# Three turns of normalised rows held back by order edges on TensorE, and the final norm's weights multiplied in together with its scaling on half the columns

## The chip, the cores and the metric

The kernel runs on one core of one Trainium2 chip. The metric is the device time of one execution in microseconds. The engines are TensorE (PE in the profile; PEld is its weight load), VectorE (DVE), ScalarE (ACT), GpSimd (POOL) and SyncE (SP); DMAs are issued from SP, ACT and POOL.

## The reference, cut to what matters

A decoder layer on 256 tokens of 1024 features in float32: an FFN, a token mixer and a second FFN, each behind a norm that is shifted and scaled by a conditioning vector, each added to the residual stream `h` with a gate, and a norm at the end.

```python
def rmsnorm(x, g):
    y = xf * lax.rsqrt(jnp.mean(xf * xf, axis=-1, keepdims=True) + EPS)
    return (y * g.astype(jnp.float32)).astype(x.dtype)

def modulate(n, shift, scale):
    return n * (1 + scale) + shift

def swiglu(n, w_gate, w_up, w_down):
    return (jax.nn.silu(n @ w_gate) * (n @ w_up)) @ w_down

        n = modulate(rmsnorm(h, g_ffn1[l]), sh1, sc1)
        h = h + 0.5 * gt1 * swiglu(n, w1_gate[l], w1_up[l], w1_down[l])
        n = modulate(rmsnorm(h, g_mix[l]), sh2, sc2)
        h = h + gt2 * hybrid_mixer(n, w_in[l], w_pool[l], pool_scale[l], w_out[l])
        n = modulate(rmsnorm(h, g_ffn2[l]), sh3, sc3)
        h = h + 0.5 * gt3 * swiglu(n, w2_gate[l], w2_up[l], w2_down[l])
    return rmsnorm(h, g_final)
```

The mixer projects the normed rows with `w_in`, feeds half the columns to causal pooling and the rest to dilated attention, and projects the result with `w_out`.

## The kernel before, in words

The 256 tokens are two token tiles of 128 rows, t = 0 and 1. `h` lies in SBUF with tokens on the partitions, 1024 columns per tile.

**Products.** A float32 product is made as three products of rounded parts: each weight half of 1024 columns is cast to `hi` on ScalarE (L289) and the remainder to `lo` on VectorE (L290), each activation is split into a high part (`nh`, `hh`, `nhy`) and a low part (`nl`, `hl`, `nly`), and high x hi, low x hi, high x lo are added up in PSUM. Weights come in one stream of 1 MB tiles that SP issues (L273); `want` fetches up to five tiles ahead of the products (`AHEAD`). The conditioning matrix comes in the same stream, and VectorE reduces it (L278).

**The norms in the middle.** When the last product of a tile's accumulator pair has run, `norm_rows` multiplies both accumulators with the gate (L331), adds them to `h` (L333), sums the squares on ScalarE (L336) and VectorE (L339), takes the power -0.5 on GpSimd (L342), and scales the rows into two tiles `xs`, the first on ScalarE (L344), the second on VectorE (L345). Then `norm_mod` turns the rows on TensorE (`turn`, L317: 4 transposes for each half), and ScalarE writes the scaled and shifted columns as `nh` (L363) and `n32` (L364), from which VectorE makes `nl` (L366). This happens four times: for t = 0 and 1 after the first FFN (tags `b0`, `b1`) and after the mixer (tags `c0`, `c1`).

**Where the turns stand.** While tile 0's norm is made, TensorE works on tile 1, and the other way round. The turn of `b0` is recorded among the down products of tile 1 (`ffn_rest`, L509, ahead of the last chunk, `TURN = 3`), that of `c0` among tile 1's products of `w_out` (`wout`, L796), that of `c1` among tile 0's first FFN products (L838), that of `b1` among tile 0's second chunk of the mixer's projection (L775, `AFTER1`). The framework's scheduler then orders each engine's queue by priority and by its own estimate of when things are ready; `norm_mod` runs under a high priority (`urgent`), so it may draw a turn ahead of products recorded before it. An engine works through its queue in the order that the built program gives it. `order_dep(late, early)` adds an edge that only the scheduler sees: `late` gets its place behind `early`, without a semaphore.

**The end.** `finish3(t)` makes the last norm for a tile. `add` multiplies the accumulator with the gate into the scratch `o` (L856) and adds it to `h` (L857). For tile 1 the last 256 columns have a second part, `far` (L444, L869). `square` takes squares and their sum on ScalarE (L861), adds on GpSimd (L862), and multiplies `h` with the final norm's weights `gfb` into `o` (L863). VectorE squares the last 256 columns (L871), GpSimd takes the power (L874), VectorE multiplies the last columns with the weights meanwhile (L875). Then `o` is scaled by the power: columns 0 to 192 and 192 to 640 on VectorE (L877), 640 to 1024 on ScalarE (L879), and three DMAs carry them out (L878 from SP, L880 from ACT). Tile 0's end runs beside tile 1's last products; tile 1's comes after everything.

Of the kernel before, what the change touches and what calls it, by code (L numbers as in the profile page):

```python
# [15 lines left out]
P = 128  # L16
S = 256
NT = S // P
D = 1024
# [26 lines left out]
SPIN = (4, 8, 8, 5)  # L46
SPLIT = (9, 10)
PARTS = 11
PAD = 336
# [122 lines left out]
def block_kernel(ctx, tc, w, vec, x, c, gf, wpool, bandd, biasd, out):  # L172
# [139 lines left out]

    def turn(src, name):

        pt = psp.tile([P, 4, P], F32, name=name, tag="ps")
        for i in range(4):
            nc.tensor.transpose(pt[:, i, :], src[:, ts(i, P)], ident)  # L317
        return pt
# [30 lines left out]

    def norm_mod(xs, which, shm, tag, t=None, xT=None):  # L350

        nh, nl = new_n(tag)
        with urgent(), in_order() as last:
            for b in range(2):
                pt = turn(xs[b], f"xt{tag}{b}")
                if xT is not None and b == 1:
# [69 lines left out]
    def down(f, ci, t, hid, accs, banks=(0, 1)):  # L426
        hi, lo = want("down", (f, ci))
        hh, hl = hid
        for k in range(2):
            first, last = ci == 0 and k == 0, ci == NCH - 1 and k == 1  # L430
            for (a, ww, st, sp) in ((hh, hi, first, False), (hl, hi, False, False), (hh, lo, False, last)):
                for b in banks:
                    mm(accs[b], a[:, k, :], cols(ww, 2 * k + b), start=st, stop=sp)  # L433

# [32 lines left out]
    def lead_step(f, j, n, items, banks, tt=range(NT)):  # L467

        hi, lo = want("lead", (f, j))
        passes = ((0, hi), (1, hi), (0, lo))  # L470
        end = KD - 1 if f == 1 else KD // 2 - 1
        if j % (end + 1) < end:
            steps = [(p, ci, t) for p in range(3) for ci in items for t in tt]
        else:
            steps = [(p, ci, t) for ci in items for t in tt for p in range(3)]
        for p, ci, t in steps:
            a, ww = passes[p]
            last = j == KD - 1 or (ci, j) in ((2, end), (3, end))
            mm(banks[ci][t], n[t][a][:, j, :], cols(ww, lead_set(f, j).index(ci)), start=j == 0 and p == 0,  # L479
               stop=last and p == 2)  # L480

# [5 lines left out]
    def ffn_rest(f, ci0, n, prev, pci, accs, finish, gate):  # L487
# [17 lines left out]
        down(f, NCH - 1, 0, hid[NCH - 1][0], accs[0])  # L505
        after = finish(0)
        for banks in ((0, 1),) if f == 0 else ((0,), (1,)):
            for ci in last:
                if after and ci == last[TURN]:  # L509
                    after()  # L510
                if f == 0 or banks == (0,) or ci < SPLIT[0]:
                    down(f, ci, 1, hid[ci][1], accs[1], banks)
        if f == 1:
# [118 lines left out]
    def finish1(t):  # L632
        with urgent():
            if t == 0:
                scale_cols(1, SC2)
            xs = norm_rows(t, f"b{t}", nm["acc"][t], nm["g"],
                           (place["win", (1, 1)] + 0.5 if t == 0 else place["win", (3, 0)], place["win", (1, 0)] + 1))
        def after():
            nm[t] = norm_mod(xs, 1, SH2, f"b{t}")
            if t == 1:  # L640
# [152 lines left out]

    def wout(t, banks, after=None):
        for n, i in enumerate(WOUT):
            if after and n == TURN1:  # L796
                after()
            hi, lo = want("wout", i)
            yh, yl = y[t]
            for kk in range(2):  # L800
                k = 2 * i + kk
                for (a, ww, st, sp) in ((yh, hi, n + kk == 0, False), (yl, hi, False, False),
                                        (yh, lo, False, n == 3 and kk == 1)):
                    for b in banks:
                        mm(acc2[t][b], a[:, k, :], cols(ww, 2 * kk + b), start=st, stop=sp)  # L805

    n3 = {}

    def finish2(t):
        with urgent():  # L810
            if t == 0:
# [3 lines left out]
                           (place["lead", (1, 4)], place["lead", (1, 2)]))  # L815
        def after():
            n3[t] = norm_mod(xs, 2, SH3, f"c{t}", t, xT3)
            if t == 1:
# [15 lines left out]
    for t in range(NT):  # L834
        for ci in range(LEAD):
            lead[ci][t] = (psp if ci > 1 else accp).tile([P, 512], F32, name=f"le{t}{ci}", tag="ps" if ci > 1 else "acc")
        for j in range(KD // 2):
            if t == 0 and j == TURN2:  # L838
                after()
            lead_step(1, j, n3, range(LEAD), lead, (t,))  # L840
    for j in range(KD // 2, KD):
# [7 lines left out]
    def finish3(t):  # L849
        with urgent():  # L850
# [3 lines left out]

            def add(src, a, b):
                nc.vector.tensor_tensor(o[:, a:b], src, g[:, a:b], ALU.mult)  # L856
                nc.vector.tensor_tensor(ht[:, a:b], ht[:, a:b], o[:, a:b], ALU.add)  # L857

            def square(n, a, b, more):
                sq = work.tile([P, 512], F32, name=f"sqo{t}{a}", tag="t2", bufs=T2)  # L860
                nc.scalar.activation(sq[:, 0:b - a], ht[:, a:b], AF.Square, accum_out=ss[:, n:n + 1])  # L861
                nc.gpsimd.tensor_tensor(ss[:, n:n + 1], ss[:, n:n + 1], more, ALU.add)  # L862
                nc.vector.tensor_tensor(o[:, a:b], ht[:, a:b], gfb[:, a:b], ALU.mult)  # L863
# [10 lines left out]
            nc.gpsimd.tensor_tensor(r, ss[:, 2:3], mhalf, ALU.pow)  # L874
            nc.vector.tensor_tensor(o[:, 768:D], ht[:, 768:D], gfb[:, 768:D], ALU.mult)  # L875
            for a, b in ((0, 192), (192, 640)):
                nc.vector.tensor_scalar(o[:, a:b], o[:, a:b], r, None, ALU.mult)  # L877
                nc.sync.dma_start(out[t * P:(t + 1) * P, a:b], o[:, a:b])  # L878
            nc.scalar.activation(o[:, 640:D], o[:, 640:D], AF.Copy, scale=r)  # L879
            nc.scalar.dma_start(out[t * P:(t + 1) * P, 640:D], o[:, 640:D])  # L880

# [40 lines left out]
```

## Time and profile before

| | |
|---|---|
| median of 3 runs | 486.09 us (485.42 to 486.2) |
| the profiled execution | 485.93 us |
| its span, first to last instruction | 484.1 us |
| mean granted TensorE clock | 0.997 |
| busy: PE, DVE, ACT, POOL | 472.5, 357.8, 261.7, 14.9 us |

In the rows of a timeline the first number is the start in us from the span's start, the second the length, then engine, line, operation, output<-inputs, sizes and count; in brackets stand the idle time of the engine just before it and what ended it. Several like instructions are merged (x8). Matmuls are pipelined, so a row may be longer than the distance to the next one.

### The profile page before, as it was taken

The page shows a single profiled execution, that of the slowest core. Times are in us where ns is not written, and L with a number is a line of the kernel's source. Part 1 is how long each engine was busy: PE and PEld are TensorE (multiplying, and loading weights), DVE is VectorE, ACT ScalarE, POOL GpSimd, SP SyncE. Part 2 cuts the span into 40 slices and gives each one's busy share as a digit, 9 for nine tenths or more (in the row PEclk, how much of TensorE's full clock was granted, in tenths as well). Part 3 has the DMA queues.
Part 4 walks back from the last instruction along what each step waited for, and adds up shares of the span by engine and source line. Part 5 has one row for each costly group of instructions (what it writes and reads, how often), then busy time and mean ns, then how long its engine had stood idle before and what let it go on. Part 6 is the DMA issues. An engine that isn't in the chain of part 4 may idle for free.

```text
span 484.1 us, 6040 instructions
## 1 busy us (share of the span) xinstructions
PE 472.5 (98%) x2188; PEld 382.6 (79%) x2188; DVE 357.8 (74%) x579; ACT 261.7 (54%) x447; POOL 14.9 (3%) x35
## 2 busy tenths in 40 slices
PE   8999999999999999999999999999999999999994
PEld 4778888888888888788778777888878888888883
DVE  4988899996897893699999869866576765655245
ACT  3786595453464451996876388746543643444111
POOL 2000000000000000110001000000000000000010
PEclk9999999999999999999999999999999999999998
DMA  8998895998988791679786963996356757530102
GB/s 303 400 347 348 330 366 191 359 417 330 376 319 328 296 383 79 236 253 383 286 339 238 339 253 104 367 347 227 135 214 260 262 202 319 208 141 0 43 1 87
DMA packets 19215, 126.05 MB, mean 260 GB/s; under 512 B 2329, under 2 KB 3121, under 8 KB 4850
## 3 DMA queue, kind: packets, MB, share of 16 engines
q1 hardware_dynamic: 17568, 121.25, 65.9%
q0 software_dynamic: 1184, 3.98, 2.3%
q10 hardware_dynamic: 434, 0.45, 0.3%
q8 instruction: 17, 0.28, 0.2%
q14 instruction: 12, 0.10, 0.0%
HBM read 124.61 MB, written 1.06 MB: 260 GB/s over the span
## 4 chain that ended last, share of the span: by engine, by line
PE 91%; DVE 3%; ACT 2%; issue 1%; DMA 1%; POOL 1%; POOLq 0%; DVEq 0%; ACTq 0%
PE accf L433 23%; PE gu L394 9%; PE gu L392 9%; PE gu L393 9%; PE le L479 8%; PE ld L479 8%; PE accm L805 4%; PE zp L392 3%; PE zp L394 3%; PE zp L393 3%; PE ht L419 2%; PE yt L731 1%; DMA h<-in_x_dram 1%; PE sh L394 1%; PE ld L394 1%
## 5 line engine op out<-in xcount | busy, mean ns | idle before, releaser
L290 DVE TENSOR_TENSOR lo<-raw,hi 128x1024 fp32r<-128x1024 f32 (+1 forms) x156 | 184.2, 1208 | 43.1 <-ACT hi L289 34.7
L289 ACT CAST hi<-raw 128x1024 fp32r<-128x1024 f32 (+1 forms) x156 | 158.7, 1047 | 70.0 <-DMA raw<-in_w_dram 28.5
L278 DVE CUSTOM_DVE_ANT_0 raw<-raw,cb,vecs 128x1024 f32<-128x1024 f32 x70 | 88.2, 1280 | 1.2 <-DMA raw<-in_w_dram 1.2
L433 PE MATMUL accf<-hi,hh 128*128 128x512 f32 x172 | 54.5, 394 | 0.2
L433 PE MATMUL accf<-hi,hl 128*128 128x512 f32 x172 | 54.4, 391 | 0.0
L433 PE MATMUL accf<-lo,hh 128*128 128x512 f32 x172 | 53.9, 389 | 0.0
L392 PE MATMUL gu<-hi,nhc 128*128 128x512 f32 x112 | 44.4, 396 | 0.0
L410 ACT ACTIVATE sg<-gu 128x256 f32<-128x256 f32 x24 | 9.2, 382 | 64.4 <-PE gu L394 64.4
L394 PE MATMUL gu<-lo,nhc 128*128 128x512 f32 x112 | 43.7, 390 | 0.0
L393 PE MATMUL gu<-hi,nlc 128*128 128x512 f32 x112 | 43.6, 389 | 0.0
L433 PEld LDWEIGHTS accf<-hi,hl 128*128 128x128 f32 x172 | 32.1, 188 | 7.2 <-DVE hl L310 0.7
L433 PEld LDWEIGHTS accf<-lo,hh 128*128 128x128 f32 x172 | 32.3, 188 | 6.8
L433 PEld LDWEIGHTS accf<-hi,hh 128*128 128x128 f32 x172 | 31.7, 188 | 7.2 <-ACT hh L309 1.1
L413 DVE TENSOR_TENSOR pr<-sg,gu 128x256 f32<-128x256 f32 x24 | 10.1, 419 | 33.0 <-ACT sg L410 32.8
L392 PE MATMUL gu<-hi,nha 128*128 128x512 f32 x80 | 31.7, 396 | 0.0
L394 PE MATMUL gu<-lo,nha 128*128 128x512 f32 x80 | 31.2, 390 | 0.0
L393 PE MATMUL gu<-hi,nla 128*128 128x512 f32 x80 | 31.1, 389 | 0.0
L310 DVE TENSOR_TENSOR hl<-ht,hh 128x256 fp32r<-128x256 f32 x44 | 16.4, 418 | 14.4 <-ACT hh L309 14.4
L309 ACT CAST hh<-ht 128x256 fp32r<-128x256 f32 x44 | 14.1, 379 | 23.0 <-PE ht L419 23.0
L392 PE MATMUL zp<-hi,nhb 128*128 128x512 f32 x64 | 26.3, 411 | 0.0
L394 PE MATMUL zp<-lo,nhb 128*128 128x512 f32 x64 | 25.3, 395 | 0.0
L393 PE MATMUL zp<-hi,nlb 128*128 128x512 f32 x64 | 25.1, 392 | 0.0
(194 smaller groups left out, 729.4 us busy)
## 6 DMA issues: line engine op xcount, KB each, us to landing
raw<-in_w_dram SPq DMA_DIRECT2D x112, 1024.0 KB, 5.9
raw<-in_w_dram SPq DMA_DIRECT2D x4, 512.0 KB, 7.8
gt<-gd POOLq DMA_DIRECT2D x3, 512.0 KB, 6.7
h<-in_x_dram SPq DMA_DIRECT2D x2, 512.0 KB, 4.6
bias<-in_bias_dram POOLq DMA_DIRECT2D x2, 512.0 KB, 3.4
band_all<-in_band_dram POOLq DMA_DIRECT2D x1, 544.0 KB, 3.8
gfb<-in_gf_dram POOLq DMA_DIRECT2D x1, 512.0 KB, 12.8
out_dram<-o SPq DMA_DIRECT2D x2, 224.0 KB, 2.4
```

The lines of the kernel that those rows point to most:

```text
L278: note(nc.vector.tensor_tensor_reduce(r, r, cb, 1.0, vecs[:, m:m + 1], ALU.mult, ALU.add, mod[:, m:m + 1]), i, 1)
L289: note(nc.scalar.copy(hi[:, o:o + n], src), i + s / 2, 0)
L290: note(nc.vector.tensor_tensor(lo[:, o:o + n], src, hi[:, o:o + n].bitcast(F32), ALU.subtract), i + s / 2, 0)
L309: nc.scalar.copy(hi_ap, src)
L310: nc.vector.tensor_tensor(lo_ap, src, hi_ap.bitcast(F32), ALU.subtract)
L392: mm(ps, nh[:, k, :], whi, start=first, stop=False)
L393: mm(ps, nl[:, k, :], whi, start=False, stop=False)
L394: mm(ps, nh[:, k, :], wlo, start=False, stop=last)
L413: nc.vector.tensor_tensor(pr, sg, ps[:, 256:512], ALU.mult)
L433: mm(accs[b], a[:, k, :], cols(ww, 2 * k + b), start=st, stop=sp)
L479: mm(banks[ci][t], n[t][a][:, j, :], cols(ww, lead_set(f, j).index(ci)), start=j == 0 and p == 0, stop=last and p == 2)
L805: mm(acc2[t][b], a[:, k, :], cols(ww, 2 * kk + b), start=st, stop=sp)
```

## The change

`turn` takes a list of matmuls and ties each of its transposes behind the 26th of them (`GATE = 25`). `ffn_rest`, `wout` and the first loop of the second FFN collect the products that they issue (`down`, `lead_step` and `wout` now keep them), and hand the list to the turns of `b0`, `c0` and `c1`. `b1`'s turn gets no list (`after(steps=())`). In `finish3` the sum of columns 512 to 1024 is made in two instructions of 256, the products with `gfb` for columns 512 to 1024 are gone, and the last scaling takes them in: VectorE makes `h` x power x `gfb` for columns 512 to 768 and 768 to 1024 in one instruction each, ScalarE scales columns 0 to 512, and the DMAs follow those columns.

```diff
+GATE = 25
...
-    def turn(src, name):
+    def turn(src, name, steps=()):
...
-            nc.tensor.transpose(pt[:, i, :], src[:, ts(i, P)], ident)
+            one = nc.tensor.transpose(pt[:, i, :], src[:, ts(i, P)], ident)
+            if steps:
+                order_dep(one.ins, steps[GATE].ins, "rows are ready later")
...
-                pt = turn(xs[b], f"xt{tag}{b}")
+                pt = turn(xs[b], f"xt{tag}{b}", steps)
...
+        steps = []
         for banks in ((0, 1),) if f == 0 else ((0,), (1,)):
             for ci in last:
                 if after and ci == last[TURN]:
-                    after()
+                    after(steps)
                 if f == 0 or banks == (0,) or ci < SPLIT[0]:
-                    down(f, ci, 1, hid[ci][1], accs[1], banks)
+                    steps += down(f, ci, 1, hid[ci][1], accs[1], banks)
...
-            def add(src, a, b):
+            def add(src, a, b, pieces=1):
                 nc.vector.tensor_tensor(o[:, a:b], src, g[:, a:b], ALU.mult)
-                nc.vector.tensor_tensor(ht[:, a:b], ht[:, a:b], o[:, a:b], ALU.add)
+                for i in range(pieces):
+                    q = slice(a + (b - a) // pieces * i, a + (b - a) // pieces * (i + 1))
+                    nc.vector.tensor_tensor(ht[:, q], ht[:, q], o[:, q], ALU.add)
...
-                nc.vector.tensor_tensor(o[:, a:b], ht[:, a:b], gfb[:, a:b], ALU.mult)
...
-            add(nm["acc"][t][1], 512, D)
+            nc.vector.tensor_tensor(o[:, 0:512], ht[:, 0:512], gfb[:, 0:512], ALU.mult)
+            add(nm["acc"][t][1], 512, D, 2)
...
-            nc.vector.tensor_tensor(o[:, 768:D], ht[:, 768:D], gfb[:, 768:D], ALU.mult)
-            for a, b in ((0, 192), (192, 640)):
-                nc.vector.tensor_scalar(o[:, a:b], o[:, a:b], r, None, ALU.mult)
+            for a, b in ((512, 768), (768, D)):
+                nc.vector.scalar_tensor_tensor(o[:, a:b], ht[:, a:b], r, gfb[:, a:b], ALU.mult, ALU.mult)
                 nc.sync.dma_start(out[t * P:(t + 1) * P, a:b], o[:, a:b])
-            nc.scalar.activation(o[:, 640:D], o[:, 640:D], AF.Copy, scale=r)
-            nc.scalar.dma_start(out[t * P:(t + 1) * P, 640:D], o[:, 640:D])
+            nc.scalar.activation(o[:, 0:512], o[:, 0:512], AF.Copy, scale=r)
+            nc.scalar.dma_start(out[t * P:(t + 1) * P, 0:512], o[:, 0:512])
```

TensorE's queue at the turn of `b0` (`xtb`, from the rows `xsb`), among tile 1's down products of the first FFN (`accf`), before:

```order
L433 MATMUL accf_852<-hi_1_1448,hh_8_1_1504 128x512
L433 MATMUL accf_851<-hi_1_1448,hl_8_1_1505 128x512
L317 MATMUL xtb_1799<-ident,xsb_1757 128x128 x4
L317 MATMUL xtb_1815<-ident,xsb_1758 128x128 x4
L433 MATMUL accf_852<-hi_1_1448,hl_8_1_1505 128x512
L433 MATMUL accf_851<-lo_1_1449,hh_8_1_1504 128x512
```

And in the changed kernel, where every line number past the edited places is larger:

```order
L438 MATMUL accf_852<-hi_1_1448,hh_8_1_1504 128x512
L438 MATMUL accf_851<-hi_1_1448,hl_8_1_1505 128x512
L438 MATMUL accf_852<-hi_1_1448,hl_8_1_1505 128x512
L438 MATMUL accf_851<-lo_1_1449,hh_8_1_1504 128x512
L438 MATMUL accf_852<-lo_1_1449,hh_8_1_1504 128x512
L438 MATMUL accf_851<-hi_0_1470,hh_9_1_1608 128x512
L438 MATMUL accf_852<-hi_0_1470,hh_9_1_1608 128x512
L318 MATMUL xtb_1799<-ident,xsb_1757 128x128 x4
L318 MATMUL xtb_1815<-ident,xsb_1758 128x128 x4
```

Five products now run ahead of this turn that ran behind it. At the turns of `c0` and `c1` (`xtc`) it is seven in the same way; what they turn is unchanged, and the turn of `b1` keeps its place.

ScalarE's queue at the turn of `c1`: the row `xsc`, casts of weights (`hi` from `raw`) and the scalings of the turned rows (`nhc`, `n32c` from `xtc`), before:

```order
L344 ACTIVATE xsc_2732<-h,rc_2730 128x512
L289 CAST hi_0_2609<-raw_2607 128x1024
L363 ACTIVATE nhc_2806<-xtc_2808,mod,acol 128x128
L364 ACTIVATE n32c_2813<-xtc_2808,mod,acol 128x128
L363 ACTIVATE nhc_2806<-xtc_2808,mod,acol 128x128
L364 ACTIVATE n32c_2813<-xtc_2808,mod,acol 128x128
```

And in the changed kernel:

```order
L347 ACTIVATE xsc_2732<-h,rc_2730 128x512
L290 CAST hi_0_2609<-raw_2607 128x1024
L290 CAST hi_1_2613<-raw_2607 128x1024
L367 ACTIVATE nhc_2806<-xtc_2808,mod,acol 128x128
L368 ACTIVATE n32c_2813<-xtc_2808,mod,acol 128x128
L367 ACTIVATE nhc_2806<-xtc_2808,mod,acol 128x128
```

The cast of the second half of the same weight tile (`hi_1_2613`) now stands ahead of the eight scalings; before, it stood behind them and the copy of the other half's turn. VectorE's `lo` of that half moves along with it. The queues around `b0`, `b1` and `c0` keep their order on ScalarE and VectorE.

VectorE's queue at the end of tile 1, from the product of the second accumulator with the gate on (`o` is the scratch, `far` the second part of the last columns, `sso` the sums of squares, `ro` the power), before:

```order
L856 TENSOR_TENSOR o_4186<-accf_3206,gt_3955 128x512
L857 TENSOR_TENSOR h<-h,o_4186 128x512
L863 TENSOR_TENSOR o_4186<-h,gfb 128x256
L856 TENSOR_TENSOR o_4186<-far,gt_3955 128x256
L857 TENSOR_TENSOR h<-h,o_4186 128x256
L871 ISA o_4186,sso_4187<-h,sso_4187 128x256
L871 ISA sso_4187 128x1
L875 TENSOR_TENSOR o_4186<-h,gfb 128x256
L877 TENSOR_SCALAR o_4186<-o_4186,ro_4203 128x192
L877 TENSOR_SCALAR o_4186<-o_4186,ro_4203 128x448
```

And in the changed kernel:

```order
L867 TENSOR_TENSOR o_4185<-accf_3206,gt_3955 128x512
L870 TENSOR_TENSOR h<-h,o_4185 128x256 x2
L867 TENSOR_TENSOR o_4185<-far,gt_3955 128x256
L870 TENSOR_TENSOR h<-h,o_4185 128x256
L884 ISA o_4185,sso_4186<-h,sso_4186 128x256
L884 ISA sso_4186 128x1
L889 SCALAR_TENSOR_TENSOR o_4185<-h,ro_4202,gfb 128x256 x2
```

The products of `h` with `gfb` for columns 512 to 1024 are gone, the first sum is two instructions, and the last row stands for two instructions that read the power and the weights.

More of the change, by code (lines that the diff above doesn't have):

```diff
@@ L348, in norm_rows, with norm_mod @@
         return xs
-    def norm_mod(xs, which, shm, tag, t=None, xT=None):
+    def norm_mod(xs, which, shm, tag, t=None, xT=None, steps=()):
         nh, nl = new_n(tag)
@@ L432, in down @@
                 for b in banks:
-                    mm(accs[b], a[:, k, :], cols(ww, 2 * k + b), start=st, stop=sp)
+                    steps.append(mm(accs[b], a[:, k, :], cols(ww, 2 * k + b), start=st, stop=sp))
+        return steps
     def down_halves(f, chunks, hid, acc_b, other):
@@ L475, in lead_step @@
             steps = [(p, ci, t) for ci in items for t in tt for p in range(3)]
+        done = []
         for p, ci, t in steps:
@@ L478, in lead_step @@
             last = j == KD - 1 or (ci, j) in ((2, end), (3, end))
-            mm(banks[ci][t], n[t][a][:, j, :], cols(ww, lead_set(f, j).index(ci)), start=j == 0 and p == 0,
-               stop=last and p == 2)
+            done.append(mm(banks[ci][t], n[t][a][:, j, :], cols(ww, lead_set(f, j).index(ci)), start=j == 0 and p == 0,
+                           stop=last and p == 2))
+        return done
     def lead_out(f, banks, chunks):
@@ L506, in ffn_rest @@
         after = finish(0)
+        steps = []
         for banks in ((0, 1),) if f == 0 else ((0,), (1,)):
@@ L637, in finish1, with after @@
                            (place["win", (1, 1)] + 0.5 if t == 0 else place["win", (3, 0)], place["win", (1, 0)] + 1))
-        def after():
-            nm[t] = norm_mod(xs, 1, SH2, f"b{t}")
+        def after(steps=()):
+            nm[t] = norm_mod(xs, 1, SH2, f"b{t}", steps=steps)
             if t == 1:
@@ L794, in wout @@
     def wout(t, banks, after=None):
+        steps = []
         for n, i in enumerate(WOUT):
             if after and n == TURN1:
-                after()
+                after(steps)
             hi, lo = want("wout", i)
@@ L804, in wout @@
                     for b in banks:
-                        mm(acc2[t][b], a[:, k, :], cols(ww, 2 * kk + b), start=st, stop=sp)
+                        steps.append(mm(acc2[t][b], a[:, k, :], cols(ww, 2 * kk + b), start=st, stop=sp))
     n3 = {}
@@ L815, in finish2, with after @@
                            (place["lead", (1, 4)], place["lead", (1, 2)]))
-        def after():
-            n3[t] = norm_mod(xs, 2, SH3, f"c{t}", t, xT3)
+        def after(steps):
+            n3[t] = norm_mod(xs, 2, SH3, f"c{t}", t, xT3, steps)
             if t == 1:
@@ L836, in block_kernel @@
             lead[ci][t] = (psp if ci > 1 else accp).tile([P, 512], F32, name=f"le{t}{ci}", tag="ps" if ci > 1 else "acc")
+        steps = []
         for j in range(KD // 2):
             if t == 0 and j == TURN2:
-                after()
-            lead_step(1, j, n3, range(LEAD), lead, (t,))
+                after(steps)
+            steps += lead_step(1, j, n3, range(LEAD), lead, (t,))
     for j in range(KD // 2, KD):
```

## The prediction

> **What bounds the kernel now.** I read the page first, then the waits by engine, then a table of the stretches of the span, then the timeline around each wait and at the end.
>
> The page's first line, its chain of waits by engine, and a line of the list of TensorE's waits (us in all, times, the longest):
>
> ```profile
> span 484.1 us, 6040 instructions
> PE 91%; DVE 3%; ACT 2%; issue 1%; DMA 1%; POOL 1%; POOLq 0%; DVEq 0%; ACTq 0%
> PE xtc L317 <- ACT xsc L344: 1.4, 2, 0.7
> ```
>
> TensorE's own work is 91% of the chain that ended last, so what it does not compute is what can be won. The table of stretches (length, then busy time of PE, PEld, DVE, ACT, POOL, granted clock, DMA share, GB/s) shows where that is:
>
> ```profile
> 12.00:190.00 178.00, 177.91 (x806) 145.88 (x806) 148.97 (x224) 97.03 (x149) 1.29 (x2) 1.00 0.86 331
> 190.00:207.00 17.00, 16.27 (x76) 13.17 (x75) 11.95 (x21) 12.41 (x27) 3.31 (x8) 1.00 0.50 187
> 207.00:276.00 69.00, 69.00 (x365) 53.99 (x364) 63.49 (x141) 49.78 (x111) 2.18 (x4) 1.00 0.81 309
> 276.00:297.00 21.00, 19.56 (x94) 15.82 (x93) 14.78 (x22) 14.73 (x30) 1.48 (x4) 1.00 0.48 175
> 297.00:475.00 178.00, 177.85 (x807) 146.43 (x806) 108.47 (x152) 82.37 (x124) 2.81 (x6) 1.00 0.53 195
> ```
>
> From 12 to 475 us TensorE is idle for more than 0.15 us in two stretches only, 0.73 and 1.44 us, and the clock is full everywhere. The 1.44 are the two xtc waits of the list, the 0.73 an xtb wait like them: the turns of a token tile's rows stand in TensorE's queue before the rows exist. The timeline at the first of them, after the first FFN:
>
> ```profile
> 193.64 0.61 PE L433 MATMUL accf<-hi,hh 128*128 128x512 f32 x2
> 194.10 0.39 PE L433 MATMUL accf<-hi,hl 128*128 128x512 f32 x1
> 194.44 0.72 ACT L344 ACTIVATE xsb<-h,rb 128x512 f32<-128x512 f32 x1 [1.80 <-POOL rb L342]
> 195.21 1.09 PE L317 MATMUL xtb<-ident,xsb 128*128 128x128 f32 x8 [0.73 <-ACT xsb L344]
> ```
>
> Two products start in 0.46 us (193.64 to 194.10), so one takes 0.23. The turn would have started at 194.33 and started at 195.21: 0.88 us lost, a little more than the 0.73 counted as idle, because the product before it drains its pipeline meanwhile. ScalarE's row ends at 195.16, and TensorE goes on 0.05 us later. The other two places:
>
> ```profile
> 280.40 0.39 PE L805 MATMUL accm<-hi,nhy 128*128 128x512 f32 x1
> 281.51 1.09 PE L317 MATMUL xtc<-ident,xsc 128*128 128x128 f32 x8 [0.72 <-ACT xsc L344]
> 292.68 0.84 PE L479 MATMUL le<-hi,nlc 128*128 128x512 f32 x3
> 294.24 1.09 PE L317 MATMUL xtc<-ident,xsc 128*128 128x128 f32 x8 [0.71 <-ACT xsc L344]
> ```
>
> 280.40 + 0.23 = 280.63 against 281.51, and 292.68 + 3 x 0.23 = 293.36 against 294.24: 0.88 us each. Together the waits cost 2.64 us.
>
> **The edges.** The order of the built program puts 5, 7 and 7 more products ahead of the three turns, worth 1.13, 1.59 and 1.59 us. The rows are then late by 0.88 less that, so they are early by 0.25, 0.70 and 0.70 us, and all three waits end: -2.64 us. The rows' own chain starts from the last product of the accumulator before, which the edges don't move.
>
> What the later turn delays: at the first place ScalarE has three weight casts queued between its row and the first scaling of the turn, so a turn that starts 0.25 us later by the rows' clock costs nothing. At the third place a cast now stands ahead of the scalings; that is priced as a rival below.
>
> What is late next: there is a fourth turn of this kind, that of token tile 1 for the mixer, and no edge holds it. It stands behind the projection's first products, and its rows pass through ScalarE:
>
> ```profile
> 203.40 1.14 ACT L289 CAST hi<-raw 128x1024 fp32r<-128x1024 f32 x1
> 203.47 1.29 DVE L333 TENSOR_TENSOR h<-h,resb 128x512 f32<-128x512 f32 x2
> 204.34 0.72 ACT L336 ACTIVATE resb<-h 128x512 f32<-128x512 f32 x1
> 206.96 0.72 ACT L344 ACTIVATE xsb<-h,rb 128x512 f32<-128x512 f32 x1 [0.88 <-POOL rb L342]
> 208.26 0.60 PE L317 MATMUL xtb<-ident,xsb 128*128 128x128 f32 x4
> ```
>
> The square (L336) has no idle time before it: it waits for ScalarE, which is working through the tile 0 scalings and this cast, not for VectorE's sum, whose first half ends near 204.15. When TensorE is 0.88 us ahead, VectorE's sums come 0.88 earlier but ScalarE's queue does not, so the square stays at 204.34 and the rows at 206.96 + 0.72 = 207.68. TensorE would reach the turn at 208.26 - 0.88 = 207.38 and can go at 207.68 + 0.05 = 207.73: 0.35 us comes back as a new wait. Its bounds are 0 (ScalarE's queue comes forward after all) and 0.88. Sum of the edges: -2.64 + 0.35 = -2.29.
>
> **The last norm.** What runs from the last product to the last transfer:
>
> ```profile
> 476.45 0.69 DVE L857 TENSOR_TENSOR h<-h,o 128x512 f32<-128x512 f32 x1
> 476.84 0.28 PE L444 MATMUL far<-lo,hh 128*128 128x256 f32 x1
> 477.18 0.42 DVE L863 TENSOR_TENSOR o<-h,gfb 128x256 f32<-128x256 f32 x1
> 477.52 0.42 DVE L856 TENSOR_TENSOR o<-far,gt 128x256 f32<-128x256 f32 x1
> 477.97 0.43 DVE L857 TENSOR_TENSOR h<-h,o 128x256 f32<-128x256 f32 x1
> 478.54 0.48 DVE L871 CUSTOM_DVE_ANT_0 o<-h,sso 128x256 f32<-128x256 f32 x1
> 479.07 0.43 DVE L875 TENSOR_TENSOR o<-h,gfb 128x256 f32<-128x256 f32 x1
> 479.11 0.79 POOL L874 TENSOR_TENSOR ro<-sso,mhalf 128x1 f32<-128x1 f32 x1 [1.09 <-DVE sso L871]
> L342 POOL TENSOR_TENSOR rb<-vb,mhalf x2: 559/560/560, 193.8 to 206.4; 128x1 f32<-128x1 f32 x2
> 479.94 0.61 ACT L879 ACTIVATE o<-o,ro 128x384 f32<-128x384 f32 x1 [2.25 <-POOL ro L874]
> 479.94 0.68 DVE L877 TENSOR_SCALAR o<-o,ro 128x192 f32<-128x192 f32 x2 [0.44 <-POOL ro L874]
> 480.28 0.81 SPq L878 DMA_DIRECT2D out_dram<-o  x2
> 480.58 0.39 ACTq L880 DMA_DIRECT2D out_dram<-o  x1
> out_dram<-o SPq DMA_DIRECT2D x1, 224.0 KB, 2.4
> out_dram<-o ACTq DMA_DIRECT2D x1, 192.0 KB, 2.1
> ```
>
> The 512-wide sum becomes two of 256 that start 0.34 us apart (as 477.18 to 477.52), the second ending at 476.45 + 0.34 + 0.43 = 477.22. The product with the far columns overwrites the scratch which that sum reads, so it starts at 477.25 (TensorE is done at 477.12) instead of 477.52: -0.27, which is the removed weight product less the split. Sum, squares and power follow at their old distances, the power at 478.84.
>
> The power took 0.79 us with VectorE's product of two SBUF tensors (L875) beside it, and 0.56 at L342, where VectorE waited. L875 is gone and VectorE waits there now, so I take 0.56: done at 479.40, and the scalings start at 479.44 instead of 479.94. If 0.79 belongs to the line itself, 0.23 of this is lost.
>
> The Trainium skill's page "SBUF — State Buffer", section "Who interferes with whom", says that a GpSimd instruction which reads SBUF contends with a VectorE instruction that has two SBUF inputs. By that rule the 0.23 goes; the two rows agree with it.
>
> ScalarE scales 512 columns instead of 384: 0.72 as L344 for 0.61, so its transfer is issued at 480.19 instead of 480.58. VectorE's two scalings of 256 with the weights have no row; the nearest are the two-tensor products of 256 (0.43), the bounds 0.32 (half of L877's pair, rounded down) and 0.48 (L871). With 0.43 SP issues first at 479.89 instead of 480.28 and again 0.39 us earlier. All three issues come 0.39 earlier, and they move the same 512 KB, so I take -0.39 for the last landing. The ends: the 256 KB transfer as quick as the 192 KB one gives 480.19 + 2.1 = 482.29 against 483.1 now (SP's pair of issues ends at 481.09 and one takes about 0.39, so the second starts at 480.70; with 2.4), -0.8; a power of 0.79 and 0.3 us more for the larger transfer, as from 192 to 224 KB, give about 0. Tile 0's end changes alike and has VectorE's pause before tile 1's last product to hide in.
>
> The page "DMA: Bandwidth & Descriptors" of the Trainium skill, section "Anatomy of one DMA — SWDGE (gpsimd) path", fits 2.0 us plus the bytes at 436 GB/s. That speaks against a larger last transfer: an estimate by it is 2.6 us for 256 KB, landing at 482.79, and the tail would win 0.32. The 2.4 and 2.1 us of the trace decide here.
>
> **The sum.** -2.64 + 0.35 - 0.39 = -2.68 us. The profiled execution took 485.93 us, 1.83 around its span of 484.1; it would be 483.25. The median of the three runs is 486.09, 0.16 above it; I say 483.3. A change under 0.2%, 1.0 us, can't be told from none here.
>
> **The rivals.**
>
> 1. The fourth turn does not wait, because ScalarE's queue comes forward too. For it: the cast at 203.40 is bulk work, and the trace does not show what released it. Against it: no idle time stands before it or before the square. -2.64 - 0.39 gives 483.0.
>
> 2. A further wait takes one of the three gains. The tightest place:
>
> ```profile
> 204.67 0.76 DVE L366 TENSOR_TENSOR nlb<-n32b,nhb 128x256 fp32r<-128x256 f32 x2
> 205.24 0.41 PE L393 MATMUL zp<-hi,nlb 128*128 128x512 f32 x1
> ```
>
> The first of these two nlb instructions ends near 205.09, 0.15 us before its product (204.67 + 0.42, as a product of 256 takes at 477.18). It stays ahead only because the sums in front of it on VectorE, which TensorE releases, come forward with TensorE. If they don't, up to 0.88 us returns: 484.2.
>
> 3. Slower: at the third place the cast of the next weights' second half now stands in ScalarE's queue ahead of the eight scalings of tile 1.
>
> ```profile
> 295.03 0.45 ACT L363 ACTIVATE nhc<-xtc,mod,acol 128x128 fp32r<-128x128 f32 x1
> 301.80 0.84 PE L479 MATMUL le<-hi,nhc 128*128 128x512 f32 x3
> ```
>
> A cast costs about 1.1 us (203.40, above), so the first scaled column is there at 295.03 + 1.1 + 0.45 = 296.6, and TensorE asks for it at 301.80 - 0.88 = 300.9. It decides from 4.3 us of lateness on, and only from 4.3 + 2.7 + 1.0 = 8.0 us is the kernel measurably slower, at 487.1 or more. That needs a cast held for its weights; against it, the cast just ahead of it reads the same tile.
>
> 4. The edges do nothing, since the wait moves with the turn: only the tail is left, 485.7. Against it: the rows' chain starts from an earlier product, and 1.13 us is more than 0.88.
>
> **How the numbers follow.** The forecast has 0.66, rival 1 0.14, rival 2 0.13, rival 3 0.03, rival 4 0.04. Faster by over 0.2% are the first three, 0.93; within it rival 4, 0.04; slower rival 3, 0.03. The range takes rivals 1 and 2 with the tail's ends (483.0 - 0.43, and 484.2 with the tail a little under its value): 482.5 to 484.4.
>
> **What would show it.** The list of TensorE's waits should have no xtc row and an xtb row of about 0.2 to 0.4 us, now for tile 1's turn (near 207.7). The stretch from 276 to 297 should have TensorE full. The power at the end should take 0.56, and the last landing should come 5.6 us after the last product ends, now 6.0. An xtc wait that remains, a wait at zp or le, or a power of 0.79 would prove a step wrong.

## The result and the profile after

The changed kernel takes 483.19 us (median of 5 runs, 482.93 to 484.57) against 486.09 us before in the same set (485.42 to 487.02). The ratio is 0.9947, its 95% interval 0.9936 to 0.9958. The forecast was 483.3 us.

The profiled execution has a span of 481.2 us against 484.1 and took 483.05 us. The table of stretches of the changed kernel, with the columns as before (length, then busy time of PE, PEld, DVE, ACT and POOL, granted clock, DMA share, GB/s):

```profile
190.00:207.00 17.00, 17.00 (x79) 13.71 (x78) 11.95 (x22) 12.85 (x27) 3.73 (x8) 1.00 0.53 192
207.00:276.00 69.00, 68.72 (x363) 53.79 (x363) 63.31 (x142) 49.28 (x111) 1.74 (x4) 1.00 0.82 311
276.00:297.00 21.00, 21.00 (x103) 17.56 (x102) 15.89 (x24) 16.03 (x32) 1.49 (x4) 1.00 0.50 181
```

TensorE is now full in the two stretches that had 0.73 and 1.44 us of idle time, and has 0.28 us of idle time in the stretch between them, which was full. The list of TensorE's waits names that one, and has no row for `xtc` any more:

```profile
PE xtb L318 <- ACT xsb L347: 0.3, 1, 0.3
```

The timeline at the turn of `b0` (195.03 us) and at that of `b1` (207.30 us), with what ScalarE does ahead of the second:

```profile
194.58 0.62 PE L438 MATMUL accf<-hi,hh 128*128 128x512 f32 x2
195.03 1.03 PE L318 MATMUL xtb<-ident,xsb 128*128 128x128 f32 x8
...
202.97 1.13 ACT L290 CAST hi<-raw 128x1024 fp32r<-128x1024 f32 x1
203.91 0.72 ACT L339 ACTIVATE resb<-h 128x512 f32<-128x512 f32 x1
206.52 0.72 ACT L347 ACTIVATE xsb<-h,rb 128x512 f32<-128x512 f32 x1 [0.87 <-POOL rb L345]
206.63 0.39 PE L397 MATMUL zp<-hi,nlb 128*128 128x512 f32 x1
207.30 1.09 PE L318 MATMUL xtb<-ident,xsb 128*128 128x128 f32 x8 [0.28 <-ACT xsb L347]
```

At `b0` two products of 0.23 us follow 194.58 and the turn starts at 195.03, without a wait. At `b1` it could have started at 206.63 + 0.23 = 206.86 and starts at 207.30, when the row that ends at 206.52 + 0.72 = 207.24 is there: 0.44 us lost start to start. The square (L339) again has no idle time before it.

The end of the changed kernel, from the last product on:

```profile
474.08 0.28 PE L450 MATMUL far<-lo,hh 128*128 128x256 f32 x1
474.55 0.42 DVE L867 TENSOR_TENSOR o<-far,gt 128x256 f32<-128x256 f32 x1
476.14 0.55 POOL L887 TENSOR_TENSOR ro<-sso,mhalf 128x1 f32<-128x1 f32 x1 [1.16 <-DVE sso L884]
476.73 0.72 ACT L891 ACTIVATE o<-o,ro 128x512 f32<-128x512 f32 x1 [2.08 <-POOL ro L887]
476.73 0.88 DVE L889 SCALAR_TENSOR_TENSOR o<-h,ro,gfb 128x256 f32<-128x256 f32 x2 [0.66 <-POOL ro L887]
477.24 0.81 SPq L890 DMA_DIRECT2D out_dram<-o  x2
477.48 0.35 ACTq L892 DMA_DIRECT2D out_dram<-o  x1
```

And the transfers that these issue, with KB each and the time from issue to landing; the last issue, SP's second, is at 477.67:

```profile
out_dram<-o ACTq DMA_DIRECT2D x1, 256.0 KB, 2.2
out_dram<-o SPq DMA_DIRECT2D x1, 128.0 KB, 2.6
```

The power is down from 0.79 to 0.55 us. From the start of the last product (476.84 before, 474.08 now) SP's first issue came after 3.44 us and comes after 3.16, ScalarE's after 3.74 and now 3.40. But the last landing, SP's second transfer at 480.22, comes after 6.15 us where it came after 6.28.

Part of the profiled execution's lead isn't the change. The first products of the second weight tile, before and after the change:

```profile
19.28 0.97 PE L479 MATMUL ld<-hi,nha 128*128 128x512 f32 x3
```

```profile
18.86 1.20 PE L486 MATMUL ld<-hi,nha 128*128 128x512 f32 x4 [0.81 <-ACT nha L464]
```

Nothing that the change touches has run by then, and this execution is 0.42 us ahead. The lead goes back to the first power on GpSimd, which ScalarE's scaling of the first rows waits for; VectorE's pass over tile 1's rows is beside it, before and after the change:

```profile
6.28 1.22 DVE L553 CUSTOM_DVE_ANT_0 xs<-h 128x1024 f32<-128x1024 f32 x1
6.30 1.62 POOL L555 TENSOR_TENSOR rx<-vx,mhalf 128x1 f32<-128x1 f32 x1 [4.96 <-DVE vx L553]
```

```profile
6.16 0.55 POOL L564 TENSOR_TENSOR rx<-vx,mhalf 128x1 f32<-128x1 f32 x1 [4.82 <-DVE vx L562]
6.72 1.23 DVE L562 CUSTOM_DVE_ANT_0 xs<-h 128x1024 f32<-128x1024 f32 x1 [0.71 <-DMA h<-in_x_dram]
```

Before, VectorE's pass started 0.02 us ahead of the power, which then took 1.62 us. After, tile 1's rows landed 0.44 us later, the pass started behind the power, and the power took 0.55. In 4 of this study's 14 profiled executions it takes about 1.6 us, and these 4 reach the second weight tile at 19.28 to 19.64 us, the others at 18.65 to 18.89. Kernels that are equal up to there show both. The two profiles without the edges are among the 4; whether it happens more often there isn't known. At the last product the changed kernel is 2.77 us ahead, so the edges made 2.35 us. With the tail's 0.13 that is the whole difference of the spans, 2.9 us.

### The profile page after: what moved, and what is told of

Read it like the earlier page. It is cut to its first block, busy times and chain, and to the rows that moved or that the text cites. A ratio compares the mean times of both kernels' runs of the same rounds, so it can differ in the third digit from the quotient of the medians.

```text
span 481.2 us, 6035 instructions
## 1 busy us (share of the span) xinstructions
PE 471.5 (98%) x2188; PEld 382.2 (79%) x2188; DVE 356.1 (74%) x577; ACT 261.3 (54%) x447; POOL 13.4 (3%) x35
## 4 chain that ended last, share of the span: by engine, by line
PE 90%; DMA 3%; ACT 3%; issue 1%; DVE 1%; POOL 0%; POOLq 0%; DVEq 0%
PE accf L438 22%; PE gu L396 9%; PE gu L398 9%; PE gu L397 9%; PE le L486 9%; PE ld L486 8%; PE accm L815 5%; PE zp L396 3%; PE zp L398 3%; PE zp L397 3%; DMA raw<-in_w_dram 3%; PE ht L423 2%; ACT hi L290 1%; PE yt L740 1%; DMA h<-in_x_dram 1%
```

## The experiments

My theory: the three waits end for 0.88 us each, the fourth turn gives 0.4 back because ScalarE's queue holds its rows, and the tail is worth a few tenths at most. The rivals: the edges do little and the start and the tail made the gain; or the tail does nothing and the edges everything.

### The edges alone

The changed kernel with the old last norm:

```diff
-            add(nm["acc"][t][1], 512, D, 2)
+            add(nm["acc"][t][1], 512, D)
...
-            for a, b in ((512, 768), (768, D)):
-                nc.vector.scalar_tensor_tensor(o[:, a:b], ht[:, a:b], r, gfb[:, a:b], ALU.mult, ALU.mult)
+            nc.vector.tensor_tensor(o[:, 768:D], ht[:, 768:D], gfb[:, 768:D], ALU.mult)
+            for a, b in ((0, 192), (192, 640)):
+                nc.vector.tensor_scalar(o[:, a:b], o[:, a:b], r, None, ALU.mult)
```

> The changed kernel with the old last norm: the order edges alone. Theory (each of three waits of TensorE of 0.88 us ends, the fourth turn gives about 0.4 back): 2.2 to 2.3 us under the kernel before, so 483.8 us; no xtc row among TensorE's waits, an xtb row of 0.3 to 0.5 us for tile 1; the tail from the last product to the last landing as in the kernel before (6.0 us). Rival A (the gain is an early start of the run and the tail, not the edges): 485.5 us or more. Rival B (the tail gives nothing at all, the edges are the whole 2.9 us): 483.2 us.

Measured: 483.09 us (482.96 to 483.83, 5 runs) against 485.76 before, ratio 0.9947 (0.9933 to 0.9961): 2.7 us, with an interval from 1.9 to 3.3 that holds both the 2.3 and the 2.9. Its waits hold a row that the changed kernel's profile doesn't have:

```profile
PE tk L318 <- ACT z L690: 0.6, 1, 0.6
PE xtb L318 <- ACT xsb L347: 0.3, 1, 0.3
```

In this profile the last product is 2.11 us ahead of the kernel before: the start gives 0.53, the turns about 2.35, and 0.77 is lost at `tk`. The edges carry the gain, so rival A falls. The `tk` row is taken up below.

### The last norm alone

The kernel before with the new last norm, no edges; shown against the changed kernel:

```diff
-    def turn(src, name, steps=()):
+    def turn(src, name):
...
-            if steps:
-                order_dep(one.ins, steps[GATE].ins, "rows are ready later")
```

> The kernel before with the new last norm alone, no edges. Theory as predicted (issues 0.39 us earlier, landing with them): 485.7 us. Theory as the trace of the changed kernel has it (issues 0.28 to 0.33 earlier, last landing only 0.13 earlier): 485.95 us. Rival B of the run with the edges alone (nothing): 486.1 us. The three waits of 0.88 us before the turns of b0, c0 and c1 stay as in the kernel before.

Measured: 485.85 us (485.19 to 486.62, 11 runs) against 485.76, ratio 1.0002 (0.9994 to 1.0011). The waits before the three turns are as they were, and the end reads like the changed kernel's, with the power at 0.55:

```profile
PE xtc L317 <- ACT xsc L344: 1.4, 2, 0.7
```

```profile
478.95 0.55 POOL L876 TENSOR_TENSOR ro<-sso,mhalf 128x1 f32<-128x1 f32 x1 [1.16 <-DVE sso L873]
```

So the faster tail is real up to the issues, and nothing of it can be told in the time. A gain of 0.13 us is inside the interval; 0.39 is just outside (0.9994 x 485.76 is 0.29 less).

### Turns held five products less

```diff
-GATE = 25
+GATE = 20
```

> The changed kernel with the turns held behind product 20 instead of 25, so five products fewer (0, 2 and 2 products ahead of the places that the kernel before has, instead of 5, 7 and 7). Theory (a wait shrinks by 0.23 us for each product put ahead until it is gone): b0 waits 0.88 us again in start to start, c0 and c1 0.42 us each, and the fourth turn waits no longer (0.44 us less), so 1.3 us over the changed kernel: 484.5 us. Rival (that the turn is held at all is what counts): 483.2 us. Rival (short holds do nothing): 485.7 us.

Measured: 484.56 us (484.36 to 485.62, 11 runs), ratio 0.9979 (0.9970 to 0.9988). The four turns in its timeline:

```profile
194.61 1.09 PE L318 MATMUL xtb<-ident,xsb 128*128 128x128 f32 x8 [0.72 <-ACT xsb L347]
207.68 1.03 PE L318 MATMUL xtb<-ident,xsb 128*128 128x128 f32 x8
280.93 1.09 PE L318 MATMUL xtc<-ident,xsc 128*128 128x128 f32 x8 [0.27 <-ACT xsc L347]
293.22 1.09 PE L318 MATMUL xtc<-ident,xsc 128*128 128x128 f32 x8 [0.26 <-ACT xsc L347]
```

`b0` has its whole wait back, `c0` and `c1` wait 0.27 and 0.26 us (0.42 start to start with the 0.15 that the pipeline hides), and `b1` waits no longer. Each product put ahead takes 0.23 us off a wait until it is gone, and the fourth turn's wait exists only because the first one went.

### The fourth turn held too

The projection's products are collected as the other stages' are, and the turn of `b1` goes behind the 28th of them instead of the 26th:

```diff
+GATE4 = 27
...
-    z["k0"] = zchunk(2, 0, 1.0, {AFTER1: after, 5: turn_heads("q0", qT, 0)})
+    z["k0"] = zchunk(2, 0, 1.0, {AFTER1: lambda: after(zsteps, GATE4), 5: turn_heads("q0", qT, 0)})
```

> The changed kernel, with the fourth turn (tile 1 before the mixer, b1) held back too, by two products (behind the 28th product of its stage instead of the 26th). Theory (the 0.44 us that it lost start to start is covered by two products, 0.46 us, and tile 1's rows aren't needed for another 5 us): 0.4 us under the changed kernel, 482.75 us, and no xtb row among TensorE's waits. Rival (the wait moves on to the first products of tile 1, or the turn's late scalings hold up ScalarE's casts): 483.2 us or more, with a new row of that wait.

Measured: 483.83 us (483.00 to 484.77, 5 runs), ratio 0.9962 (0.9949 to 0.9974): no gain. The profiled execution was the slowest of the five. Its turn of `b1` doesn't wait; the turn of tile 1's k columns does, and above it stands a cast on ScalarE:

```profile
208.18 1.08 PE L319 MATMUL xtb<-ident,xsb 128*128 128x128 f32 x8
...
227.77 1.05 ACT L291 CAST hi<-raw 128x1024 fp32r<-128x1024 f32 x1 [4.43 <-DMA raw<-in_w_dram]
228.72 0.59 ACT L692 ACTIVATE z<-zp 128x512 f32<-128x512 f32 x1
229.36 0.66 PE L319 MATMUL tk<-ident,z 128*128 128x128 f32 x4 [1.17 <-ACT z L692]
```

The eviction of `z` is ready to go, but its place in ScalarE's queue is behind a cast that waits for its weights. Their transfer was issued at 218.18 us in the changed kernel's profile and at 218.96 in this one:

```profile
raw<-in_w_dram SPq DMA_DIRECT2D x1, 1024.0 KB, 7.1
```

```profile
raw<-in_w_dram SPq DMA_DIRECT2D x1, 1024.0 KB, 8.8
```

The transfer just ahead of it on the queue, issued near 217 us, is late already. Of the 14 profiled executions of this study 8 have that one at 4.9 to 5.5 us and 6 at 6.9 to 7.5, and only profiles with the late one show the `tk` wait (0.3 to 1.2 us). The changed kernel and five of the runs here differ only in the last norm, long after it; two of these six have the transfer early, four late. It is a matter of the execution, then, and explains part of the scatter. What makes it late wasn't found.

### The turn of the k columns later as well

```diff
-    z["v0"] = zchunk(3, 0, 1.0, {3: turn_heads("k1", kT, 1), 6: sc[0]})
+    z["v0"] = zchunk(3, 0, 1.0, {5: turn_heads("k1", kT, 1), 7: sc[0]})
```

> The kernel with the fourth turn held too, and the turn of tile 1's k columns (tk) put six products later, with the first scores three products later. In the run with the fourth turn held the turn tk waited 1.2 us for ScalarE's eviction of z (L692), which stood in ScalarE's queue behind a cast that waited 4.43 us for a transfer of weights; the kernel with the edges alone showed 0.6 us there, the changed kernel none. Theory (the gain of 0.44 us at the fourth turn is real and was lost at tk, where a late transfer of weights decides): with 1.37 us more of products ahead of tk no tk row is left and the time is 0.4 us under the changed kernel, 482.75 us, with a smaller scatter than with the fourth turn held alone (483.0 to 484.8). Rival A (the stream of weights decides all of this stretch, so the wait only moves to the next consumer of late weights): 483.2 us or more, with a new row of a wait for a cast. Rival B (holding the fourth turn costs by itself): 483.8 us, without a wait in the stretch from 207 to 276 us.

Measured: 483.52 us (483.04 to 484.31, 6 runs), ratio 0.9954 (0.9940 to 0.9967). The profile has the late transfers (7.5 us, and 8.8 for the next) and no `tk` row, but a new one further on:

```profile
242.23 1.02 PE L742 MATMUL yt<-pts,z 128*64 128x256 f32 x6 [1.14 <-ACT pts L737]
```

The wait moved on, as rival A had it. The later scores aren't the cause: ScalarE, which makes the softmax and the copies `pts`, works from 231.82 to 242.56 us with one pause of 0.09 us, and it starts there with a cast that had waited 1.99 us for its weights. So `tk` was covered, and TensorE met the lateness of the weights at the next place that needs ScalarE. In the run with the edges alone, with weights as late, `pts` comes at the same time (241.55 against 241.71 us), but TensorE, held up at `tk`, gets to these products no sooner than that and shows no wait.

### Turns held eight products more

```diff
-GATE = 25
+GATE = 33
```

> The changed kernel with the turns held behind product 33 instead of 25: eight products, 1.82 us, later. The rows have long been ready. Theory (the hold is free only while the products behind the turn don't need what ScalarE and VectorE make of it): at c0 and c1 the first products that need it come 5 us and more later, so nothing is lost there; at b0 the mixer's products stand right behind, VectorE's nlb of tile 0 already ends the weight load's idle time of 0.17 us at 203.8 us in the changed kernel, so most of the 1.82 us come back there, and the time is 1.2 to 1.9 us over the changed kernel: 484.4 to 485.1 us, with rows of waits for nhb or nlb. Rival (the longer a turn is held the better or equal): 483.2 us.

Measured: 482.41 us (482.18 to 482.79, 5 runs) against 485.44, ratio 0.9932 (0.9920 to 0.9943). My theory for this run falls: nothing comes back at `b0`, and the kernel is 0.8 us under the changed one's median (0.7 by the two ratios), though the two ratios' intervals overlap. ScalarE and TensorE around the turns of `b0` and `b1`:

```profile
194.84 2.93 ACT L290 CAST hi<-raw 128x1024 fp32r<-128x1024 f32 x3
197.04 1.03 PE L318 MATMUL xtb<-ident,xsb 128*128 128x128 f32 x8
197.67 0.46 ACT L367 ACTIVATE nhb<-xtb,mod,acol 128x128 fp32r<-128x128 f32 x1
...
203.17 0.72 ACT L339 ACTIVATE resb<-h 128x512 f32<-128x512 f32 x1
...
205.80 0.73 ACT L347 ACTIVATE xsb<-h,rb 128x512 f32<-128x512 f32 x1
207.10 1.03 PE L318 MATMUL xtb<-ident,xsb 128*128 128x128 f32 x8
```

Three casts stand between `b0`'s row and its scalings, so the scalings begin at 197.67 whenever the turn comes, and the turn at 197.04 is still early enough. In the changed kernel the turn is two microseconds earlier, at 195.03, and the scalings begin no sooner, since that whole execution is 0.19 us ahead of this one here:

```profile
197.47 0.45 ACT L367 ACTIVATE nhb<-xtb,mod,acol 128x128 fp32r<-128x128 f32 x1
```

I had looked at the slack of the last `nlb`, which was nil, and not at what set its time. And something else is gone: the scheduler, planning with a later turn, put the cast at 202.97 of the changed kernel behind the square. The square is 0.74 us earlier here, the row of `b1` 0.72, and the fourth turn waits no longer. Product against product, this run gains 0.49 us on the changed kernel's profile across that turn.

### The square first

That swap alone, with the turns held behind product 25:

```diff
+                chain[tag, "square"] = nc.scalar.activation(tmp, hs, AF.Square, accum_out=v)
...
+                order_dep(casts[order[56], 0][0], chain["b1", "square"].ins, "square first")
```

> The changed kernel (turns held behind product 25) with one order edge more: on ScalarE the cast at 202.97 us in the changed kernel's profile (L290, 1.13 us) goes behind the square of tile 1's first half (L339) instead of ahead of it. The run with the hold of 33 had the same swap as a by-product, no wait at the fourth turn, and 482.41 us. Theory (the fourth turn waits because that cast stands ahead of the square): the square comes 0.7 to 0.9 us earlier, tile 1's rows with it, no xtb row is left among TensorE's waits, and the time is 482.4 to 482.8 us. Rival A (the gain of the longer hold is made at the other turns): the xtb row goes, the time stays at 483.2 us. Rival B (the cast is then late for its products): 483.2 us or more, with a wait for hi or lo between 207 and 215 us.

Measured: 483.03 us (482.28 to 483.65, 6 runs) against 485.64, ratio 0.9944 (0.9932 to 0.9956). Its timeline:

```profile
19.51 0.74 PE L486 MATMUL ld<-hi,nha 128*128 128x512 f32 x2 [0.50 <-ACT nha L464]
...
203.61 0.71 ACT L339 ACTIVATE resb<-h 128x512 f32<-128x512 f32 x1
...
207.51 1.03 PE L318 MATMUL xtb<-ident,xsb 128*128 128x128 f32 x8
```

This execution started 0.65 us later than the profiled one of the changed kernel (19.51 against 18.86 us at the products of the second weight tile), and its turn of `b1` is only 0.21 later: the 0.44 us are gone, with nothing changed but that cast's place. So the cast ahead of the square made the fourth wait. In the medians it can't be told: two runs are at 482.3, four at 482.9 to 483.7. Against the longer hold the two profiles run in step from 65 us to the end (within 0.15 us, the held turns apart), and what parts them, 0.33 us at the last product, is there before 65 us, so I can't show why that kernel's median is 0.6 lower; the intervals of the two ratios overlap.

### Why the last landing stayed

Two kernels, one run each. In the first ScalarE's transfer of tile 1 is left out (columns 0 to 511 of the last 128 rows aren't written):

```diff
+            if t == 0:
+                nc.scalar.dma_start(out[t * P:(t + 1) * P, 0:512], o[:, 0:512])
```

> The changed kernel without the transfer of ScalarE's piece of tile 1 (columns 0 to 511 of the last 128 rows aren't written; the work on them stays). It tells whether VectorE's second piece lands late because it shares the engines with ScalarE's 256 KB. Theory A (shared engines): the second piece of 128 KB lands 1.8 to 2.1 us after its issue, like the first (1.99 us), instead of 2.55, so the last landing comes 0.45 us or more earlier. Theory B (two transfers behind one another on one queue): it stays at 2.5 us. The whole time falls by as much as the last landing.

In the second VectorE's two pieces are cut at 640:

```diff
-            for a, b in ((512, 768), (768, D)):
+            for a, b in ((512, 640), (640, D)):
```

> The changed kernel with the two pieces of the last norm that VectorE scales cut at 640 instead of 768: 128 columns first (64 KB), then 384 (192 KB); ScalarE's 512 stay. Counted from the start of the last product. Theory A (the landing follows the drain of all 512 KB, which starts with the first issue): the first issue comes 0.15 us earlier, and the last landing with it, at 6.0 us instead of 6.15. Theory B (the landing follows the last issue and grows with what that piece holds): last issue as now, at 3.6 us, landing at 6.15 to 6.25 us.

SP's second transfer without ScalarE's, and with the cut at 640:

```profile
out_dram<-o SPq DMA_DIRECT2D x1, 128.0 KB, 2.0
```

```profile
out_dram<-o SPq DMA_DIRECT2D x1, 192.0 KB, 2.5
```

Without ScalarE's 256 KB the same 128 KB land 1.96 us after their issue instead of 2.55, and the last landing comes 5.56 us after the start of the last product instead of 6.15. The time is 482.45 us in one run. So SP's second transfer is later for sharing the engines with ScalarE's 256 KB; theory A holds. With the cut at 640 the first issue comes 0.13 us earlier and the last 0.03, and the last landing is at 6.09, 0.06 earlier: between the two theories.

Sharing the engines doesn't explain by itself why the landing came only 0.13 us earlier than in the kernel before, where SP's last transfer ran beside ScalarE's as well. The busy share of the DMA engines in tenths, in slices of 0.06 us that begin 4.0 us after the start of the last product, first the kernel before, then the changed one:

```profile
DMA  0000278997769999999979999899983000000000
```

```profile
DMA  5989989979998997997999895100000000000000
```

By the packets of the two traces the last one ends 5.93 us after the start of the last product before the change and 5.59 after it: 0.34 us earlier, as the issues would have it. But the landing follows that packet after 0.35 us before and after 0.56 now, which takes 0.21 back. Without ScalarE's transfer it follows after 0.55, with the cut at 640 after 0.46. These last pieces differ in the length of their rows: 1792 bytes before, 1024 in the changed kernel with and without ScalarE's transfer, 1536 with the cut at 640. Whether that sets the delay wasn't tested.

### What slows the power

A product on VectorE is put beside the power again, its result unused, once with two operands from SBUF and once, in its place, with one:

```diff
+            beside = nc.vector.tensor_tensor(du[:, 0:256], ht[:, 0:256], gfb[:, 0:256], ALU.mult)
+            order_dep(beside.ins, red.ins, "beside the power")
```

```diff
+            beside = nc.vector.tensor_scalar(du[:, 0:256], ht[:, 0:256], 2.0, None, ALU.mult)
```

> The changed kernel with a product of 128x256 on VectorE that reads two operands from SBUF (its result is used by nothing), put behind the sum of squares, so that it runs beside GpSimd's power, where the kernel before had such a product. Theory (the power is slowed by the product beside it): the power takes 0.79 us again instead of 0.55, and the scalings start 0.24 us later. Rival (the power's 0.55 us comes from elsewhere, from its own place behind the sum): 0.55 us, scalings unchanged, since the product of 0.43 us ends before them.

> The same with a scaling of 128x256 by a constant on VectorE, which reads one operand from SBUF. Theory (it is the second operand that takes GpSimd's way to the memory): the power stays at 0.55 us. Rival (any work of VectorE beside it slows the power): 0.79 us.

With two operands:

```profile
476.34 0.42 DVE L887 TENSOR_TENSOR du<-h,gfb 128x256 f32<-128x256 f32 x1
476.50 0.67 POOL L890 TENSOR_TENSOR ro<-sso,mhalf 128x1 f32<-128x1 f32 x1 [1.16 <-DVE sso L884]
```

With one:

```profile
476.73 0.29 DVE L887 TENSOR_SCALAR du<-h 128x256 f32<-128x256 f32 x1
476.89 0.55 POOL L890 TENSOR_TENSOR ro<-sso,mhalf 128x1 f32<-128x1 f32 x1 [1.16 <-DVE sso L884]
```

The product with two operands costs the power 0.12 us, not the 0.24 of the kernel before. The starts explain the difference: the power ends 0.41 us after the product here (476.76 and 477.17) and 0.40 after it there (479.50 and 479.90), as if it were held until VectorE is done. The first power of the kernel before fits too: it took 1.62 us and ended 0.42 after VectorE's pass (7.50 and 7.92). There the pass had started first, by 0.02 us; in nine runs where it starts 0.02 to 0.42 us after the power, the power takes 0.55. So the delay isn't a share of the overlap. It arises when VectorE's instruction started first, and then the power ends about 0.41 us after that instruction does.

The run with one operand doesn't decide between its theories. Its scaling ends 0.13 us after the power's start, and an undisturbed power of 0.55 ends 0.42 after that anyway. That the second operand matters isn't shown by it. Both runs took 483.5 to 483.8 us in their single executions, with a late transfer in each.

### Both edits that ended earlier

The hold of 33 and the cut at 640 together:

> The hold of 33 together with the last norm cut at 640 on VectorE, the two edits that each ended earlier than the changed kernel in their traces. Theory: the hold's 482.4 us less the 0.06 us that the cut at 640 showed from the last product to the last landing, so 482.35 us; no xtb row. Rival (a late transfer of weights near 225 us takes it back, as it did in the runs with the edges alone and with the fourth turn held): 483 us or more with a tk row of 0.6 us or more.

Measured: 482.34 us (482.05 to 482.55, 5 runs) against 485.64, ratio 0.9930 (0.9918 to 0.9942). No run of it is as slow as the fastest of the changed kernel (482.93, in its own set). Its median is the lowest of the study, 0.07 us under the hold of 33 alone in another set. The cut's 0.06 us can't be told from none.

## Why the prediction was right, point by point

- **The three waits, -2.64 us: right.** No `xtc` row is left, the stretch from 276 to 297 us is full, and five products fewer bring 0.88, 0.42 and 0.42 us back, as the counts of five, seven and seven have it. The size was a little low: taken product against product behind the turns, the waits were worth 0.92, 0.97 and 0.97 us, since a turn that waited also holds the next product 0.06 us longer (0.85 us against 0.79 after it at `c0`).
- **The fourth turn, +0.35 us: right in place and cause, 0.44 in size.** It was forecast to come at 207.7 us and came at 207.30, in an execution that is 0.42 us ahead from the start. The cause given, that the square is held by ScalarE's queue and not by VectorE's sum, was shown by moving one cast. Behind the turn it cost 0.5 us. Edges together: -2.29 forecast, -2.35 in the trace; that the sum fits so well is luck in part, as both sizes were too low and they have opposite signs.
- **The tail, -0.39 us: the step that failed.** The power went from 0.79 to 0.55 us as said. The far columns' product starts 0.21 us earlier and not 0.27, as it comes 0.11 us after the split sum ends (474.44) and not 0.03. VectorE's scaling of 256 with the weights was taken at 0.43 us and takes 0.48. So the issues come 0.28 to 0.34 earlier and not 0.39. The failing sentence is "All three issues come 0.39 earlier, and they move the same 512 KB, so I take -0.39 for the last landing": the last packet did end 0.34 earlier, but the last landing came only 0.13 earlier, 5.87 us after the last product's end and not 5.6, since it follows the last packet after 0.56 us instead of 0.35. Why it does stays open. The last norm alone made no difference that can be measured.
- **The sum.** -2.68 was forecast for the profiled execution, -2.9 came, of which 0.42 is its earlier start. Without that it would be -2.5. In the one execution the tail's error (0.26 too much) and the luck of the start (0.42 that wasn't forecast) pull against each other; the medians of the edges alone (-2.7) and of the changed kernel (-2.9 in its own set) can't settle tenths.
- **The rivals.** Rival 1 (the fourth turn doesn't wait) is refuted by its row; rival 2 (a further wait takes a gain) came in a form that I hadn't listed, the `tk` wait for late weights, in some executions and at up to 1.2 us; rival 3's cast stands ahead of the scalings at `c1` and no wait follows; rival 4 falls with the run of the edges alone.

By the Trainium skill's page "SBUF — State Buffer", section "Who interferes with whom", a GpSimd instruction that reads SBUF contends with a VectorE instruction with two SBUF inputs. The runs agree for two operands: 0.67 and 0.79 us beside them, 0.55 with nothing beside. For one operand no run here tells.

By the Trainium skill's page "DMA: Bandwidth & Descriptors", section "Anatomy of one DMA — SWDGE (gpsimd) path", 2.0 us plus the bytes at 436 GB/s is an estimate of 2.6 us for the 256 KB and 2.3 for the 128 KB. The trace has 2.2 and 2.6, so in the opposite order, and 2.0 for the 128 KB without ScalarE's. The page's fit is for one transfer on GpSimd's queue; these are issued by SP and ScalarE and share the engines.

## What to carry to other kernels

Where an in-order engine waits for rows, fill the wait with the next products by an order edge, at one product's time each, and then look for the next in-order queue on the rows' way: here a bulk cast ahead of a short square made the next wait. How late a turn may go is read from the queue of its consumer, not from the slack of the last result: it was free up to the moment at which ScalarE had worked off what stood ahead of the scalings. At the end of a kernel, issues that come earlier are worth only what the last landing gains, so read the last packet and the landing of each transfer, beside the others that share its engines.

## What the runs showed of the hardware that I had not expected

- A transfer of 1 MB issued at the same place of the program lands after 4.9 to 5.5 us in 8 profiled executions and after 6.9 to 7.5 in 6, also among kernels that are equal up to there.
- A transfer of 128 KB took 1.96 us from issue to landing behind another 128 KB, and 2.55 when 256 KB from a second queue were issued 0.2 us before it.
- The last landing followed the last packet out by 0.35 us in the kernel before, 0.46 with the cut at 640, and 0.56 in the changed kernel, or 0.55 there without ScalarE's transfer.
- When a VectorE instruction with two operands from SBUF started before GpSimd's power, by 0.02 to 0.16 us, the power ended 0.40 to 0.42 us after that instruction, and so took 0.67, 0.79 or 1.6 us. When VectorE started 0.02 to 0.42 us after it, the power took 0.55. At the start of the program that order changes from execution to execution, and 4 of 14 profiled executions are 0.4 to 1.0 us later for it at the second weight tile.
